# Output projection and beginning of a hybrid SSD and DeltaNet layer: more buffers, earlier gate rows, later halos

## The chip, the cores and the metric

The kernel runs on one core of a Trainium2 chip. The metric is the device time of one execution in microseconds (us); of several executions the median is given. The core has TensorE (PE, with its weight loads listed apart as PEld), VectorE (DVE), ScalarE (ACT), GpSimd (POOL) and SyncE (SP), which here issues most of the DMAs.

## The reference

One decoder layer on a prompt (1024 tokens) and on 64 sample tokens (8 sequences of 8), in float32. The sandwich norms, the SSD scan and the delta rule are those of the usual models; cut to what matters:

```python
mod = silu(c) @ w_ada + b_ada                      # 6 sections of 1024: sh1, sc1, g1, sh2, sc2, g2
h = rms_norm(x, norm_mix_pre) * (1 + sc1) + sh1
proj = h @ w_in                                    # z, x/B/C, dt, q/k/v, gate, beta, alpha
x/B/C, q/k/v = silu(causal_conv4(...))             # the samples bring 3 earlier columns each (halos)
y = gated_rms_norm(ssd_scan(...));  o = gated_rms_norm(delta_rule(...))
m = concat(y, o) @ w_out                           # the output projection, 2048 x 1024
x = x + g1 * rms_norm(m, norm_mix_post)
h = rms_norm(x, norm_ffn_pre) * (1 + sc2) + sh2
x = x + g2 * rms_norm((silu(h @ wg) * (h @ wu)) @ w_down, norm_ffn_post)
```

All states after the step are outputs too: the samples' delta-rule state (8 heads, 8 sequences, 128 x 128) among them.

## The kernel before

Every large product is split into high and low fp32r halves: three matmuls `hi*hi`, `hi*lo`, `lo*hi`. A weight tile of 128x512 is loaded into `wr` by SP, rounded to `wh` by ACT (L164) and its rest taken into `wl` by DVE (L165); pool `wp` has four buffers of each of the three.

The order on PE is that of the program text (a manual schedule). On the other engines and the DMA queues a planner puts the instructions in order, by readiness and priority; `tc.high_priority(n)` shifts it, a negative n backwards. Work beside the matmuls is written as Python generators: `spawn` adds one, and `tick()` lets each go on to its next `yield`, so that its instructions fall between the matmuls. `wait(n)` skips n ticks. Where a loop `while key not in box: tick()` waits, ticks pass with no matmul of the main work between them.

Stages that the change touches:

- The beginning. `ada_block(cb)` (L270) loads four `w2` tiles of 512 KB for one 512-column block of `w_ada` and multiplies them (L268); pool tile `w2` has 8 buffers, which the later `x` tiles share. Blocks 0 and 2, then 1 and 3 give shift and scale of the first norm (`ada_cols`, L287 to L292). `norm_x` (L252 to L254) normalises a row tile of x. `first_half` (L402) transposes x, applies shift and scale (`modulated`, L338 to L349), and does half of the k range of the first two weight tiles, one tick after each three matmuls in its second call. `halos` (L364) loads the samples' earlier conv columns into one buffer `vT` (ACT's queue, L369) and transposes them (L373), five times, one tick apart. `hidden_rest` does the other row tiles. `rates` (L450) multiplies the 32 narrow columns `wst` (L463), and its chain on DVE is read back by L522. `conv_tile` waits in ticks until the halos are done.
- The DeltaNet stage. `ada_rest` (L635) multiplies the other eight blocks of `w_ada`, two halves each, adds them (ACT copy L656, DVE add L658) and stores the sums, not yet folded over partitions, to DRAM (`pdr`).
- The output projection (L1656 to L1718), three groups of row tiles, 16 steps of k each; a step is two halves of 512 columns, each for three row tiles (L1335, L1337, L1338 in `gemm_rows`), with weights from `w_out_half`. Beside group 0 runs `beside`: `rows_late` loads `pdr`, folds the rows into gains (L1301) and into shift and scale of the second norm (L1313), writes the gains to DRAM (L1304) and loads them back broadcast (`load_gains`, L1270 to L1272), and loads the group norm's rates (`RB`). Then `gdn_samples` does the samples' delta rule: per head a state load `s_S` (L1498), products (L1512, L1520, L1530, L1539), the state's decay on POOL (L1527) and a store (L1546). `done` waits in ticks for `rows_late`.

Of the kernel before, what the change touches and what calls it, by code (L numbers as in the profile page):

```python
# [43 lines left out]
def hybrid_step(ctx: ExitStack, tc: tile.TileContext, x_p, x_s, c_p, c_s, st_ssd, st_ssdc, st_gdn, st_gdnc,  # L44
# [30 lines left out]
    pdr = tc.dram_tile([P, 4 * D], F32, name="pdr")  # L75
# [3 lines left out]

    ident = const.tile([P, P], F32, name="ident")  # L80
# [24 lines left out]
    sels = const.tile([P, 4, 9], F32, name="sels")  # L105
    for i in range(4):
        dve.tensor_tensor(out=sels[:, i, :], in0=fold[:, 0:9], in1=ident[:, 9 + i:10 + i].to_broadcast([P, 9]),
                          op=ALU.add)
# [27 lines left out]
    def spawn(gen):  # L136
        tasks.append(gen)
# [19 lines left out]
    def bank():  # L157
        return bg[0].tile([P, 512], F32, name="ps")


    def split_half(src, low=dve):
# [6 lines left out]
    def load_half(src, low=dve):  # L168
# [4 lines left out]
        return split_half(wr, low)  # L173
# [67 lines left out]
    def load_x(i, q=sp):  # L241
        n = P if i < NC else NS
        if i >= 4:
            xts.append(init.tile([P, 2, 512], F32, name="w2", bufs=8).rearrange("p a n -> p (a n)"))
        xt = xts[i]
        q.dma_start(out=xt[0:n], in_=x_p[i * P:(i + 1) * P, :] if i < NC else x_s)
# [22 lines left out]

    def ada_block(cb, between=None):  # L270
        ps = bank()
        for k in range(0, KD, 2):
            w2 = init.tile([P, 2, 512], F32, name="w2", bufs=8)
            sp.dma_start(out=w2, in_=w_ada[k * P:(k + 2) * P, cb * 512:(cb + 1) * 512]
                         .rearrange("(a p) n -> p a n", p=P))
# [153 lines left out]

    wsr = gk.tile([P, 4, NS], F32, name="sm").rearrange("p a t -> p (a t)").rearrange("p (k m) -> p k m", m=32)  # L430
    act.dma_start(out=wsr[:, :, 0:16], in_=w_in[:, C_DT:C_DT + 16].rearrange("(k p) m -> p k m", p=P))
    act.dma_start(out=wsr[:, :, 16:24], in_=w_in[:, C_ALPHA:C_ALPHA + 8].rearrange("(k p) m -> p k m", p=P))
    act.dma_start(out=wsr[:, :, 24:32], in_=w_in[:, C_BETA:C_BETA + 8].rearrange("(k p) m -> p k m", p=P))
    wst = gk.tile([P, NP], F32, name="gate")[:, 0:KD * 64].rearrange("p (k m) -> p k m", m=64).bitcast(F32R)
    pool.memset(wst.bitcast(F32), 0.0)
    act.copy(wst[:, :, 0:32], wsr)
    dve.tensor_sub(wst[:, :, 32:64], wsr, wst[:, :, 0:32].bitcast(F32))

# [3 lines left out]
    first_half(1)  # L442

# [10 lines left out]
    def rates():  # L454
# [180 lines left out]
    def ada_rest():  # L635

        wx = pools["wx"]
# [7 lines left out]

        w4 = load(0)
        sp.dma_start(out=pdr[9:10, :], in_=b_ada[:, 4 * 512:])
        for i in range(16):
            yield from wait(13)
            cb, hf = divmod(i, 2)  # L650
            ps = bank()
            for a in range(4):
                pe.matmul(ps[32 * a:32 * a + 32], lhsT=caF[:, 4 * hf + a, :], rhs=w4[:, a, :], start=True, stop=True)
            if hf == 0:
                pr = wx.tile([P, 512], F32, name="pr")
                act.copy(pr, ps)  # L656
            else:
                dve.tensor_tensor(out=pr, in0=ps, in1=pr, op=ALU.add)  # L658
                for r in (slice(0, 9), slice(10, P)):
                    sp.dma_start(out=pdr[r, cb * 512:(cb + 1) * 512], in_=pr[r])  # L660
            if i < 15:
                w4 = load(i + 1)

# [598 lines left out]
    ph_p = ExitStack()  # L1262
    pre = ph_p.enter_context(tc.tile_pool(name="pre", bufs=1, side="right", reuse_waits="tile"))
# [10 lines left out]
    def rows_late():  # L1274
        def rows(s):
            r = pre.tile([P, D], F32, name="rows2", bufs=2)
            sp.dma_start(out=r, in_=pdr[:, s * D:(s + 1) * D])
            return r


        r0, r1_ = rows(0), rows(1)
# [5 lines left out]
        rw = pre.tile([2 * NT, P], F32, name="rw")  # L1287
        dve.tensor_copy(rw, ps[0:2 * NT, 0:P])
        sp.dma_start(out=rsdr.rearrange("g c p -> (g c) p"), in_=rw)
        for g in range(2):  # L1290
            sp.dma_start(out=RB[g], in_=rsdr[g].rearrange("c p -> (c p)")[0:T].partition_broadcast(P))
        yield from wait(8)
        late_box["RB"] = clock[0]

        def gain_rows(i, r):
            g9 = mid.tile([P, D], F32, name="hv", bufs=5)[0:9]
            sp.dma_start(out=g9, in_=(n_mix_post, n_ffn_post)[i][0].partition_broadcast(9))
            for hf in range(2):
                cs = slice(hf * 512, hf * 512 + 512)
                ps = bank()  # L1300
                pe.matmul(ps[0:9], lhsT=sel, rhs=r[:, cs], start=True, stop=True)  # L1301
                dve.tensor_tensor(out=g9[:, cs], in0=ps[0:9], in1=g9[:, cs], op=ALU.mult)
                yield
            sp.dma_start(out=gaindr[i], in_=g9)  # L1304

        yield from gain_rows(0, r0)
        load_gains(0, GP[0], GS[0])
        r2_ = rows(2)
        ps = bank()
        pv = ps[:, 0:2 * KD * 9].rearrange("p (s k n) -> p s k n", s=2, n=9)  # L1310
        for s_, r_ in ((0, r1_), (1, r2_)):
            for k in range(KD):
                pe.matmul(pv[:, s_, k, :], lhsT=r_[:, k * P:(k + 1) * P], rhs=sel, start=True, stop=True)  # L1313
            if s_ == 0:
                r3 = rows(3)
            yield from wait(1)
        dve.tensor_copy(modT, pv)
        dve.scalar_tensor_tensor(out=modT[:, 1], in0=modT[:, 1], scalar=1.0,
                                 in1=W_FFN.unsqueeze(2).to_broadcast([P, KD, 9]), op0=ALU.add, op1=ALU.mult)
        yield from gain_rows(1, r3)  # L1320
        late_box["rows"] = clock[0]

# [87 lines left out]
    def gdn_samples():  # L1410
# [17 lines left out]
        yield from wait(3)  # L1428
# [66 lines left out]
        for h in range(HG):  # L1495
            hc = 16 + h
# [9 lines left out]
            yield from wait(1)  # L1506
# [11 lines left out]
            yield from wait(1)  # L1518
# [8 lines left out]
            pool.tensor_tensor(out=S0, in0=S0, in1=ge.to_broadcast([P, NB, P]), op=ALU.mult)  # L1527
# [33 lines left out]
    def beside():  # L1561
        yield from rows_late()
        ph_p.close()
        yield from gdn_samples()

# [20 lines left out]
    spawn(beside())  # L1586
# [72 lines left out]
    def w_out_half(k, hf):  # L1659
        return load_half(w_out[k * P:(k + 1) * P, hf * 512:hf * 512 + 512])  # L1660

    ph_f = ExitStack()
    for gi, grp in enumerate(GRP):
# [3 lines left out]
        def done(i, rows, f, hv):  # L1667
# [3 lines left out]
            while "rows" not in late_box:  # L1671
                tick()
# [241 lines left out]
```

## Time and profile before

| what | us |
|---|---|
| median of 3 runs | 2021.33 (2020.7 to 2026.5) |
| profiled execution | 2017.53 |
| its span, first to last instruction | 2015.8 |
| PE busy | 1951.3 |
| DVE busy | 1356.6 |
| ACT busy | 1014.1 |
| POOL busy | 138.7 |

The profile is of one execution. Matmuls are pipelined and overlap in the records, so a busy PE can still be slowed by its clock or by small waits. In a row of the waits the figures are the total in us, the number of waits and the longest.

### The profile page before, as it was taken

How to read it: one execution, taken by the hardware profiler on the slowest of the kernel's cores; microseconds unless marked ns; L12 is line 12 of the kernel's file. 1: busy time of each engine (PE TensorE's matmuls, PEld its weight loads, DVE VectorE, ACT ScalarE, POOL GpSimd, SP SyncE). 2: the span in 40 equal slices, each digit the busy share in tenths (PEclk: the TensorE clock that was granted, in tenths of full speed). 3: DMA queues.
4: the chain of work that ended last, by engine and by line, in shares of the span. 5: the costliest groups of instructions: out<-in, count | busy, mean ns of one | idle time of the engine just before them, and what ended most of it. 6: DMA issues, size and time to landing. Idle time of an engine off the chain costs nothing.

```text
span 2015.8 us, 35469 instructions
## 1 busy us (share of the span) xinstructions
PE 1951.3 (97%) x13211; PEld 1752.5 (87%) x13211; DVE 1356.6 (67%) x2949; ACT 1014.1 (50%) x2515; POOL 138.7 (7%) x188
## 2 busy tenths in 40 slices
PE   6999999999999999999989999999999999999998
PEld 4888999999999998998857677899999999988886
DVE  4768677877887656867648777885555556645465
ACT  3555445555555447767424556753333334444454
POOL 2110000000000001010002210100000000000000
PEclk8999999999999999999989999999999999999999
DMA  9133223333221237545376866422222223633131
GB/s 315 40 92 92 84 92 98 108 95 99 84 58 55 69 92 201 159 121 155 113 218 193 253 203 194 140 75 81 73 78 81 75 82 124 225 125 113 46 100 50
DMA packets 224764, 239.49 MB, mean 119 GB/s; under 512 B 19128, under 2 KB 177387, under 8 KB 224461
## 3 DMA queue, kind: packets, MB, share of 16 engines
q1 hardware_dynamic: 218203, 231.88, 37.2%
q10 hardware_dynamic: 6386, 5.33, 0.8%
q8 instruction: 104, 1.70, 0.4%
q14 instruction: 71, 0.58, 0.1%
HBM read 190.93 MB, written 46.25 MB: 118 GB/s over the span
## 4 chain that ended last, share of the span: by engine, by line
PE 79%; DVE 9%; DMA 6%; ACT 3%; issue 2%; POOL 0%; SPq 0%; DVEq 0%; POOLq 0%; ACTq 0%
PE ps L189 8%; PE ps L190 8%; PE ps L191 8%; PE ps L1815 7%; PE ps L1817 7%; PE ps L1816 7%; PE ps L1335 7%; PE ps L1338 6%; PE ps L1337 6%; PE ps L671 2%; PE ps L725 1%; DMA L<-accr 1%; DVE tm L827 1%; DVE rr L829 1%; DMA mx<-mixdr 1%
## 5 line engine op out<-in xcount | busy, mean ns | idle before, releaser
L189 PE MATMUL ps<-hh,wh 128*128 128x384 f32 (+1 forms) x1232 | 436.2, 354 | 0.0
L190 PE MATMUL ps<-hl,wh 128*128 128x384 f32 (+1 forms) x1232 | 403.3, 327 | 0.0
L191 PE MATMUL ps<-hh,wl 128*128 128x384 f32 (+1 forms) x1232 | 403.3, 327 | 0.0
L1335 PE MATMUL ps<-wh,sh 128*128 128x512 f32 x678 | 275.2, 406 | 7.2 <-ACT wh L164 6.4
L1338 PE MATMUL ps<-wl,sh 128*128 128x512 f32 x678 | 267.3, 394 | 3.9 <-DVE wl L165 3.8
L189 PEld LDWEIGHTS ps<-hh,wh 128*128 128x128 f32 x1232 | 232.3, 189 | 16.8 <-issue 10.4
L1337 PE MATMUL ps<-wh,sl 128*128 128x512 f32 x604 | 238.9, 395 | 0.0
L190 PEld LDWEIGHTS ps<-hl,wh 128*128 128x128 f32 x1232 | 232.4, 189 | 0.8
L191 PEld LDWEIGHTS ps<-hh,wl 128*128 128x128 f32 x1232 | 231.3, 188 | 0.0
L164 ACT CAST wh<-wr 128x512 fp32r<-128x512 f32 x200 | 123.7, 621 | 183.0 <-PE ps L190 87.6
L165 DVE TENSOR_TENSOR wl<-wr,wh 128x512 fp32r<-128x512 f32 x200 | 137.6, 693 | 66.5 <-ACT wh L164 65.8
L1335 PEld LDWEIGHTS ps<-wh,sh 128*128 128x128 f32 x678 | 128.4, 189 | 49.7 <-issue 13.7
L165 DVE TENSOR_TENSOR wl<-wd,wh 128x512 fp32r<-128x512 f32 x130 | 89.6, 692 | 118.0 <-ACT wh L164 114.7
L1338 PEld LDWEIGHTS ps<-wl,sh 128*128 128x128 f32 x678 | 128.4, 189 | 35.2 <-DVE wl L165 6.3
L164 ACT CAST wh<-wd 128x512 fp32r<-128x512 f32 x130 | 80.7, 621 | 138.9 <-PE ps L1337 100.7
L1337 PEld LDWEIGHTS ps<-wh,sl 128*128 128x128 f32 x604 | 114.7, 190 | 21.3
L1815 PE MATMUL ps<-T_0h,wh 128*128 128x272 f32 x352 | 102.2, 290 | 4.3 <-DVE u L1831 1.8
L1752 ACT CAST wh<-s 128x512 fp32r<-128x512 f32 x104 | 64.3, 620 | 78.2 <-PE ps L1816 72.6
L1817 PE MATMUL ps<-T_0h,wl 128*128 128x272 f32 x352 | 102.0, 290 | 0.7 <-DVE wl L1753 0.7
L1815 PE MATMUL ps<-T_1h,wh 128*128 128x272 f32 x352 | 102.1, 290 | 0.0
L1816 PE MATMUL ps<-T_0l,wh 128*128 128x272 f32 x352 | 101.5, 288 | 0.0
L1817 PE MATMUL ps<-T_1h,wl 128*128 128x272 f32 x352 | 101.5, 288 | 0.0
(490 smaller groups left out, 4372.8 us busy)
## 6 DMA issues: line engine op xcount, KB each, us to landing
wr<-in_w_in_dram SPq DMA_DIRECT2D x104, 256.0 KB
wr<-in_w_gate_up_dram SPq DMA_DIRECT2D x104, 256.0 KB
wr<-in_w_out_dram SPq DMA_DIRECT2D x96, 256.0 KB
w<-in_w_ada_dram SPq DMA_DIRECT2D x16, 1024.0 KB
wd<-in_w_down_dram SPq DMA_DIRECT2D x22, 512.0 KB
actdr<-as SPq DMA_DIRECT2D x18, 544.0 KB
L<-accr SPq DMA_DIRECT2D x16, 544.0 KB
am<-actdr SPq DMA_DIRECT2D x44, 192.0 KB
```

Source lines behind the costliest of these rows:

```text
L164: act.copy(wh, src)
L165: low.tensor_tensor(out=wl, in0=src, in1=wh.bitcast(F32), op=ALU.subtract)
L189: pe.matmul(out, lhsT=hi[k], rhs=xh[k], start=(k == 0), stop=False)
L190: pe.matmul(out, lhsT=hi[k], rhs=xl[k], start=False, stop=False)
L191: pe.matmul(out, lhsT=lo[k], rhs=xh[k], start=False, stop=(k == KD - 1))
L1335: pe.matmul(o, lhsT=sh[:, cs], rhs=wh, start=first, stop=False)
L1337: pe.matmul(o, lhsT=sl[:, cs], rhs=wh, start=False, stop=False)
L1338: pe.matmul(o, lhsT=sh[:, cs], rhs=wl, start=False, stop=last)
L1752: act.copy(wh, opa[p])
L1815: pe.matmul(o, lhsT=wh[:, cs], rhs=bh[:, m, :], start=(m == 0 and not on), stop=False, **on)
L1816: pe.matmul(o, lhsT=wh[:, cs], rhs=bl[:, m, :], start=False, stop=False, **on)
L1817: pe.matmul(o, lhsT=wl[:, cs], rhs=bh[:, m, :], start=False, stop=(m == 3), **on)
```

## The change

In the beginning, `w2` gets 12 buffers and the loads are issued ahead in the order block 0, block 2, first weight halves, block 1, and block 3 after block 0's products; a tiny Silu comes first on ACT; the normalising of the later x tiles gets a lower priority; the halos' transposes come three ticks after their load; the narrow weight columns are loaded by SP after `first_half(1)` instead of by ACT before it, and split inside `rates`. In the DeltaNet stage `ada_rest` folds each block at once, into gains (`gaindr`) or into `modT`, with the bias added on DVE; `pdr` is gone. In the output projection odd k take weights from a second pool `wo` of three buffers; `rows_late` keeps only the gains' loads and `RB`, the latter now on POOL's queue; `gdn_samples` starts beside it, issues each head's state load and copies one head ahead, and scales the state on ACT, 8 instructions per head.

```diff
-    sels = const.tile([P, 4, 9], F32, name="sels")      # and 8 instead of 4 in its loop
+    warm = const.tile([1, 1], F32, name="warm")
+    dve.memset(warm, 0.0)
+    act.activation(out=warm, in_=warm, func=AF.Silu)
...
+    def load_ada(cb):                                   # the loads of ada_block, w2 with bufs=12
...
     def halos():
             act.dma_start(out=st, in_=src[:, :, a * P:(a + n) * P].rearrange("b t c -> (b t) c"))
+            yield from wait(3)
             ps = bank()
...
     def hidden_rest():
-        for i in range(3, NT):
-            norm_x(i)
+        with tc.high_priority(-80):
+            for i in range(3, NT):
+                norm_x(i)
...
+    load_ada(0)
+    load_ada(2)
+    for load in loads:
+        load(0)
+    load_ada(1)
     rows = ada_block(0)
+    load_ada(3)
     for i in range(3):
         norm_x(i)
     rows2 = ada_block(2, lambda: ada_cols(0, rows))
-    for load in loads:
-        load(0)
...
     first_half(1)
+    wsr = gk.tile([P, 4, NS], F32, name="sm")...
+    sp.dma_start(out=wsr[:, :, 0:16], in_=w_in[:, C_DT:C_DT + 16]...)     # three, were on act before first_half(1)
...
     def rates():
+        act.copy(wst[:, :, 0:32], wsr)
+        dve.tensor_sub(wst[:, :, 32:64], wsr, wst[:, :, 0:32].bitcast(F32))
+        yield from wait(2)
...
     def ada_rest():
+        b8 = wx.tile([P, 512], F32, name="b8")
+        pool.memset(b8, 0.0)
+        sp.dma_start(out=b8[9:17, :], in_=b_ada[0, 4 * 512:].rearrange("(r c) -> r c", c=512))
         for i in range(16):
-            yield from wait(13)
+            yield from wait(11)
             ...
-            if hf == 0:
-                act.copy(pr, ps)
-            else:
-                dve.tensor_tensor(out=pr, in0=ps, in1=pr, op=ALU.add)
-                for r in (slice(0, 9), slice(10, P)):
-                    sp.dma_start(out=pdr[r, cb * 512:(cb + 1) * 512], in_=pr[r])
+            dve.tensor_tensor(out=pr, in0=ps, in1=pr if hf else b8, op=ALU.add)
+            if hf == 0:
+                continue
+            yield from wait(3)
+            ps = bank()
+            if sec in (0, 3):
+                pe.matmul(ps[0:9], lhsT=sels[:, cb, :], rhs=pr, start=True, stop=True)
+                dve.tensor_tensor(out=g9, in0=ps[0:9], in1=g9, op=ALU.mult)
+                sp.dma_start(out=gaindr[sec // 3][:, 512 * half:512 * half + 512], in_=g9)
+                continue
+            for a in range(4):
+                pe.matmul(pv[:, a, :], lhsT=pr[:, a * P:(a + 1) * P], rhs=sels[:, cb, :], start=True, stop=True)
+            # into modT[:, 0] or, with 1 + and the norm's weight, modT[:, 1]
...
+    wo = ph_b.enter_context(tc.tile_pool(name="wo", bufs=3, side="right", reuse_waits="tile"))
     def rows_late():
-        r0, r1_ = rows(0), rows(1)
+        load_gains(0, GP[0], GS[0])
         ...
-        sp.dma_start(out=rsdr..., in_=rw)               # RB's loads likewise
+        pool.dma_start(out=rsdr..., in_=rw)
-        yield from gain_rows(0, r0)                     # and all that follows it
...
     def gdn_samples():
-        yield from wait(3)
+        yield from wait(16)
...
+        nxt = prep(0)                                   # state load and diagonal copies of a head
+        yield from wait(2)
         for h in range(HG):
+            S0, kb = nxt
...
-            yield from wait(1)
+            if h + 1 < HG:
+                nxt = prep(h + 1)
+            yield from wait(2)
             ...
-            pool.tensor_tensor(out=S0, in0=S0, in1=ge.to_broadcast([P, NB, P]), op=ALU.mult)
+            for b in range(NB):
+                act.activation(out=S0[:, b, :], in_=S0[:, b, :], func=AF.Copy, scale=ge[:, b])
...
-    spawn(beside())
+    spawn(rows_late())
+    spawn(gdn_samples())
     def w_out_half(k, hf):
-        return load_half(w_out[k * P:(k + 1) * P, hf * 512:hf * 512 + 512])
+        return load_half(w_out[k * P:(k + 1) * P, hf * 512:hf * 512 + 512], wp=wo if k % 2 else wp)
         def done(i, rows, f, hv):
-            while "rows" not in late_box:
-                tick()
```

## Rows read from the trace of the kernel before

**Rows 1.** The page's first part: busy us, share of the span and instructions of each engine.

```profile
PE 1951.3 (97%) x13211; PEld 1752.5 (87%) x13211; DVE 1356.6 (67%) x2949; ACT 1014.1 (50%) x2515; POOL 138.7 (7%) x188
```

**Rows 2.** Waits of PE from 0 to 75 us: total us, times, longest us.

```profile
PE ps L259 <- ACT gate L229: 7.5, 1, 7.5
PE ps L373 <- DMA vT<-in_state_ssd_conv_dram: 4.5, 1, 4.5
PE ps L409 <- DVE hl L349: 3.3, 2, 2.2
PE ps L268 <- DMA w<-in_w_ada_dram: 1.7, 2, 1.4
```

**Rows 3.** Windows: busy us and instructions of PE, PEld, DVE, ACT, POOL; clock; DMA.

```profile
44.00:48.00 4.00, 4.00 (x16) 3.21 (x14) 2.33 (x7) 2.38 (x6) 2.95 (x4) 0.60 1.16 212
...
54.00:58.00 4.00, 3.96 (x23) 3.57 (x23) 2.05 (x5) 1.95 (x3) 0.39 (x1) 0.57 0.10 25
...
60.00:90.00 30.00, 29.41 (x184) 25.88 (x185) 23.38 (x56) 18.80 (x44) 7.39 (x10) 1.00 0.13 32
```

**Rows 4.** Timeline of the beginning: start us, us, instruction, idle time before it.

```profile
5.01 1.28 ACT L229 ACT_TABLE_LOAD   x1 [5.01 <-DMA gate<-in_c_sample_dram]
...
20.77 3.81 ACTq L300 DMA_DIRECT2D r<-in_norm_mix_pre_dram  x1
...
41.11 0.75 DVE L254 TENSOR_SCALAR kq<-kq,rs 128x1024 f32<-128x1024 f32 x1 [0.66 <-POOL rs L122]
...
109.19 0.59 PE L522 MATMUL ps<-s,ones 128*128 128x192 f32 x2 [2.34 <-DVE s L516]
```

**Rows 5.** Groups of the DeltaNet stage: count, busy us, mean ns, idle us before.

```profile
L658 DVE TENSOR_TENSOR pr<-ps,pr 128x512 f32<-128x512 f32 x8 | 5.4, 677 | 3.1 <-PE ps L653 3.1
```

**Rows 6.** Groups of PE in the output projection, the moved products.

```profile
L1301 PE MATMUL ps<-rows,sels 128*9 128x512 f32 x8 | 5.0, 706 | 0.0
L1313 PE MATMUL ps<-sels,rows 128*128 128x9 f32 x32 | 3.8, 255 | 1.0 <-DMA rows<-pdr 1.0
```

**Rows 7.** Waits of PE from 990 to 1266 us.

```profile
PE ps L1335 <- ACT wh L164: 6.4, 2, 6.1
PE ps L1338 <- DVE wl L165: 3.8, 2, 2.7
PE ps L1520 <- DVE s_Y L1515: 1.4, 1, 1.4
PE ps L1530 <- DVE s_ut L1522: 1.3, 1, 1.3
PE ps L1597 <- DVE s_S L1542: 1.0, 1, 1.0
```

**Rows 8.** Timeline of SP's queue in the output projection.

```profile
1026.85 6.52 SPq L1272 DMA_DIRECT2D gs<-gaindr  x8
...
1036.97 0.26 SPq L1304 DMA_DIRECT2D gaindr<-hv  x1
...
1039.31 0.84 SPq L172 DMA_DIRECT2D wr<-in_w_out_dram  x2
```

**Rows 9.** Windows of the output projection, columns as in rows 3.

```profile
1030.00:1034.00 4.00, 4.00 (x11) 1.51 (x11) 0.82 (x3) 0.00 (x0) 0.00 (x0) 0.57 0.49 161
...
1044.60:1051.00 6.40, 6.38 (x19) 4.99 (x20) 5.37 (x10) 4.54 (x14) 0.00 (x0) 0.52 0.91 301
1240.00:1247.00 7.00, 6.03 (x19) 4.80 (x20) 6.49 (x14) 2.80 (x5) 0.00 (x0) 0.76 0.58 182
```

**Rows 10.** Durations of one line, ns min/median/max: state scaling on POOL, ACT.

```profile
L1527 POOL TENSOR_TENSOR s_S<-s_S,s_eg x8: 1913/1943/2359, 1078.6 to 1172.1; 128x1024 f32<-128x1024 f32 x8
...
L1156 ACT ACTIVATE h<-h,eb x64: 385/390/414, 786.8 to 994.9; 128x128 f32<-128x128 f32 x64
```

**Rows 11.** Groups of ACT from 990 to 1266 us, the weight casts.

```profile
L164 ACT CAST wh<-wr 128x512 fp32r<-128x512 f32 x94 | 58.0, 620 | 78.6 <-PE ps L1337 33.7 <-issue 23.6 <-DMA wr<-in_w_out_dram 5.9
```

**Rows 12.** Waits of SP's queue over the span.

```profile
SPq L1498 <- DMA out_dram<-s_S: 10.8, 5, 3.2
```

More of the change, by code (lines that the diff above doesn't have):

```diff
@@ L103, in hybrid_step @@
     dve.tensor_add(fold, fold, ident[:, 96:128])
-    sels = const.tile([P, 4, 9], F32, name="sels")
-    for i in range(4):
+    sels = const.tile([P, 8, 9], F32, name="sels")
+    for i in range(8):
         dve.tensor_tensor(out=sels[:, i, :], in0=fold[:, 0:9], in1=ident[:, 9 + i:10 + i].to_broadcast([P, 9]),
@@ L158, in bank, with split_half @@
         return bg[0].tile([P, 512], F32, name="ps")
-    def split_half(src, low=dve):
+    def split_half(src, low=dve, wp=wp):
         wh = wp.tile([P, 512], F32R, name="wh")
@@ L166, in split_half, with load_half @@
         return wh, wl
-    def load_half(src, low=dve):
+    def load_half(src, low=dve, wp=wp):
         wr = wp.tile([P, 512], F32, name="wr")
@@ L172, in load_half @@
         sp.dma_start(out=wr.rearrange("p (a b) -> p a b", b=sh[2]) if len(sh) == 3 else wr, in_=src)
-        return split_half(wr, low)
+        return split_half(wr, low, wp)
     def load_tile(w, c0, low=dve):
@@ L243, in load_x @@
         if i >= 4:
[L244 removed]
+            xts.append(init.tile([P, 2, 512], F32, name="w2", bufs=12).rearrange("p a n -> p (a n)"))
         xt = xts[i]
@@ L268, in ada_rows @@
             pe.matmul(ps[r], lhsT=caF[:, k, :], rhs=w(k), start=k < 4, stop=k >= 4)
+    w2s = {}
+    def load_ada(cb):
+        w2s[cb] = []
+        for k in range(0, KD, 2):
+            w2 = init.tile([P, 2, 512], F32, name="w2", bufs=12)
+            sp.dma_start(out=w2, in_=w_ada[k * P:(k + 2) * P, cb * 512:(cb + 1) * 512]
+                         .rearrange("(a p) n -> p a n", p=P))
+            w2s[cb].append(w2)
     def ada_block(cb, between=None):
@@ L272, in ada_block @@
         for k in range(0, KD, 2):
-            w2 = init.tile([P, 2, 512], F32, name="w2", bufs=8)
-            sp.dma_start(out=w2, in_=w_ada[k * P:(k + 2) * P, cb * 512:(cb + 1) * 512]
-                         .rearrange("(a p) n -> p a n", p=P))
+            w2 = w2s[cb][k // 2]
             ada_rows(ps, lambda k: w2[:, k % 2, :], (k, k + 1))
@@ L442, in hybrid_step @@
     first_half(1)
+    wsr = gk.tile([P, 4, NS], F32, name="sm").rearrange("p a t -> p (a t)").rearrange("p (k m) -> p k m", m=32)
+    sp.dma_start(out=wsr[:, :, 0:16], in_=w_in[:, C_DT:C_DT + 16].rearrange("(k p) m -> p k m", p=P))
+    sp.dma_start(out=wsr[:, :, 16:24], in_=w_in[:, C_ALPHA:C_ALPHA + 8].rearrange("(k p) m -> p k m", p=P))
+    sp.dma_start(out=wsr[:, :, 24:32], in_=w_in[:, C_BETA:C_BETA + 8].rearrange("(k p) m -> p k m", p=P))
+    wst = gk.tile([P, NP], F32, name="gate")[:, 0:KD * 64].rearrange("p (k m) -> p k m", m=64).bitcast(F32R)
+    pool.memset(wst.bitcast(F32), 0.0)
     dcol = cA.tile([P, KD], F32, name="dcol")
@@ L644, in load @@
             return w4
+        b8 = wx.tile([P, 512], F32, name="b8")
+        pool.memset(b8, 0.0)
         w4 = load(0)
-        sp.dma_start(out=pdr[9:10, :], in_=b_ada[:, 4 * 512:])
+        sp.dma_start(out=b8[9:17, :], in_=b_ada[0, 4 * 512:].rearrange("(r c) -> r c", c=512))
         for i in range(16):
-            yield from wait(13)
+            yield from wait(11)
             cb, hf = divmod(i, 2)
+            sec, half = divmod(cb, 2)
             ps = bank()
@@ L1274, in rows_late @@
     def rows_late():
[L1275 to L1278, printed above, removed]
-        r0, r1_ = rows(0), rows(1)
+        load_gains(0, GP[0], GS[0])
         while "norm" not in rate_box:
@@ L1286, in rows_late @@
         pe.transpose(ps[0:2 * NT, 0:P], rsg.rearrange("p g c -> p (g c)"), ident)
-        rw = pre.tile([2 * NT, P], F32, name="rw")
+        rw = g_.tile([2 * NT, P], F32, name="rw")
         dve.tensor_copy(rw, ps[0:2 * NT, 0:P])
-        sp.dma_start(out=rsdr.rearrange("g c p -> (g c) p"), in_=rw)
+        pool.dma_start(out=rsdr.rearrange("g c p -> (g c) p"), in_=rw)
         for g in range(2):
-            sp.dma_start(out=RB[g], in_=rsdr[g].rearrange("c p -> (c p)")[0:T].partition_broadcast(P))
+            pool.dma_start(out=RB[g], in_=rsdr[g].rearrange("c p -> (c p)")[0:T].partition_broadcast(P))
         yield from wait(8)
         late_box["RB"] = clock[0]
[L1295 to L1304, printed above, removed]
-        yield from gain_rows(0, r0)
[L1307 to L1315, printed above, removed]
-            yield from wait(1)
[L1317 to L1321, printed above, removed]
     GRP = ((0, 1, 2), (3, 4, 5), (6, 7, 8))
@@ L1494, in gdn_samples, with prep @@
         so = small.tile([P, HG], F32, name="s_so", bufs=1)
-        for h in range(HG):
-            hc = 16 + h
+        def prep(h):
             S0 = g_.tile([P, NB, P], F32, name="s_S0", bufs=2)
@@ L1505, in gdn_samples @@
             dve.tensor_tensor(out=diag(1), in0=bt(smp[:, h, 1, :]), in1=bt(eg[:, h, :]), op=ALU.mult)
-            yield from wait(1)
+            return S0, kb
+        nxt = prep(0)
+        yield from wait(2)
+        for h in range(HG):
+            S0, kb = nxt
             pk = bank()
```

28 lines of the change are left out of this document (12 added, 16 removed).

## The prediction

> **What bounds the kernel now.** I read the page's engine shares first, then PE's waits by stage, then windows around the longest waits, last the timeline of the queue behind each wait. The shares say that PE is the bound: 1951.3 us busy of a span of 2015.8 [rows 1]. So at most some 64 us of the span are PE idle, and whatever PE does beside them has to be removed, not moved. What can be won beyond the idle time is time in which PE is busy at its lower clock. In PE's waits of the beginning the reader is to see four: 7.5 us for the first Silu, 4.5 us for a halo's load, 3.3 us for the low half of the normalised input, 1.7 us for w_ada [rows 2]. In those of the output projection: 6.4 us for a weight's high half, 3.8 us for its low half, and three of 1.0 to 1.4 us that belong to the samples' chain [rows 7]. After the long waits the granted clock lies between the two levels of 1.2 and 2.4 GHz: 0.60 and 0.57 of full speed in two stretches of the beginning [rows 3], 0.52 behind the wait at 1044 us [rows 9]. A stretch of s us with PE busy at a share c is worth (1 - c) * s.
>
> **The output projection.** (a) The rows' products leave it: L1301 is 5.0 us and L1313 3.8 us of PE [rows 6], together 8.8. They stood in front of the weights' products, so all of it counts here: -8.8.
>
> (b) SP's queue. The gains' loads start at 1026.85 and run to 1033.4; the store of the second gains goes out at 1036.97, when DVE has made them; only behind it come the weight loads, at 1039.31 [rows 8]. PE then stands 6.1 us for the cast of such a weight [rows 7] and works on at 0.52 of the clock for 6.4 us, which is 0.48 * 6.4 = 3.1 [rows 9]. Before it L1313 waited 1.0 for a row load [rows 6]. In the changed kernel the gains are in DRAM long before, so nothing on SP waits for DVE there, and RB's dependent pair is on POOL's queue. The gains' nine loads, and the samples' three, still stand on SP, some 0.4 to 0.8 us of issue each [rows 8]; at most seven buffered halves of weights, where there were four, lie over that. -1.0 - 6.1 - 3.1 = -10.2. If the cover is gone, all 10.2 stay.
>
> (c) Late weights at group changes: 0.3 us of L1335 (6.4 less 6.1) and 3.8 of L1338 [rows 7], and around the longest of them 0.24 * 7.0 = 1.7 of clock [rows 9]; together 5.8. Casts wait mostly for PE to free a buffer (33.7 of 78.6 us idle) [rows 11], so more buffers let them run ahead. But the low half is made by DVE, which at 1240 to 1247 us is busy 6.49 of 7.0 us [rows 9], and that work is not less. Two thirds: -3.9; between 0 and -5.8.
>
> (d) The samples' chain: 1.4 + 1.3 + 1.0 = 3.7 us of waits [rows 7]. It starts some 13 ticks later after its loads but no longer behind the rows, has two ticks instead of one before the first two products of each head, and is over before group 2. Half: -1.9; between -3.7 and +3.7, since a chain that meets group 0's moments can wait as much again. Preparing a head ahead adds a wait on SP: the state load of the next head needs the store of the one before last. That wait is there already, 10.8 us in five, 3.2 at the longest [rows 12], weight loads queued behind it; I cost the change of it at nothing, hidden by the buffers of (b); bare, it is 3.2 a head.
>
> (e) The state's scaling moves from POOL, 8 of 1.94 us, to ACT, 64 that should be like L1156 of the scan: 0.39 us, so 3.1 us a head and 25.0 in all [rows 10]. Weight casts of 0.62 us [rows 11] can queue behind a block. ACT is half idle [rows 1] and a cast has a lead. I take +3 for these and other new waits; between 0 and 25.
>
> Sum: -8.8 - 10.2 - 3.9 - 1.9 + 3 = -21.8.
>
> **The DeltaNet stage.** The products of (a) arrive here. In 1030 to 1034 us they ran at 0.57 of the clock [rows 9], so 1.7 of the 8.8 were clock, and here they cost 7.1: PE is the bound here too, so +7.1, between 0 (in gaps) and 8.8. DVE gets eight more adds of 0.68 [rows 5], four products of the same shape and small copies, about 9 us; ACT loses eight copies. DVE is 67% busy [rows 1], and the chain of the delta rule can be late by one add: +1.0, between 0 and 9. The DMAs to `pdr`, two per block, go from SP; a load and a store of nine partitions come for four of the blocks: nothing. Sum +8.1.
>
> **The beginning.** (f) The table load is 1.28 us in front of the Silu for which PE waits 7.5 [rows 2, 4]. ACT stands idle 5.01 us before it for the loads of c [rows 4], so the load moves into idle time. But the first product's weights are waited for just after (1.7) [rows 2], and these come no sooner: 0, between -1.3 and +1.3 (ACT issues the loads of c as well, and the table load may come ahead of them).
>
> The Trainium skill (ScalarE: Activation LUTs, What ACT_TABLE_LOAD costs) puts a switch of tables at about 1.28 us of load and 1.38 us of drain. The trace agrees on the load with its 1.28 [rows 4]; the drain no run here shows. By the page the lower end would be -2.7 and the sum 1.4 lower if the weights were early.
>
> (g) L409's waits are 3.3 us [rows 2]; in the longer one DVE does L254, 0.75 us, the normalising of a later tile, ahead of the input's low half, and ACT its square [rows 4]. With low priority these go behind: -1.5, and half of the clock loss behind it, 0.40 * 4 / 2 = 0.8 [rows 3]. Between 0 and -4.9. What is late next: the later tiles, now closer to their transposes.
>
> (h) Halos. Each load went out when the transposes before it freed `vT`, and its own transposes stood next but three matmuls on PE: 4.5 us of wait [rows 2], then 0.43 * 4 = 1.7 at 0.57 of the clock [rows 3]. With three more ticks, some 24 matmuls of the main work lie between; at the pace of 60 to 90 us, 29.41 us for 184 [rows 3], about 4 us. -4.5 - 1.7. Then PE reaches the second and third row tiles sooner than DVE has made them: a new wait, nearest L409's 3.3 [rows 2]; +2.0, between 0 and 3.3.
>
> (i) The first conv tile waits for the fifth halo, now due some 15 ticks later, so that ticks pass without matmuls and `rates` and its chain on DVE move up on PE, with two conv tiles of DVE work behind them. L522 waits 2.3 today [rows 4]: +1.0; between -2.3 and +7.5, the longest wait of this stage [rows 2].
>
> (j) Loads. Twelve `w2` buffers let block 1 go out without waiting for block 0's products, and the narrow columns no longer share the queues with it. PE meets blocks 1 and 3 only behind `first_half(0)`, where it waits 1.7 us for w_ada in all [rows 2]: 0, between -1.7 and +3.8, since a parameter load already held ACT's queue for 3.81 us [rows 4] and fuller queues can do so in front of ACT's part of the input.
>
> Sum: -2.3 - 6.2 + 2.0 + 1.0 = -5.5.
>
> **In all** -21.8 + 8.1 - 5.5 = -19.2. The profiled execution took 2017.53, of which the span is 2015.8, so it becomes 1998.3. The median of the runs shown is 2021.33, 3.8 above that execution; the forecast is for a median: 2002.1.
>
> **The rivals.**
> 1. All waits named go. Output projection -8.8 - 10.2 - 5.8 - 3.7 = -28.5; DeltaNet +7.1; beginning -3.3 - 1.6 - 4.5 - 1.7 - 2.3 = -13.4: -34.8, so 1986.5. For it: ACT and DVE have idle time on average [rows 1]. Against: at the group changes DVE has none [rows 9].
> 2. The beginning gives its waits back. The new wait of (h) is 3.3 and that of (i) 7.5: -2.3 - 6.2 + 10.8 = +2.3 there, -11.4 in all, 2009.9. For it: the halos only change place, and the ticks that the conv tile waits are empty. Against: 24 matmuls now stand between load and use.
> 3. It doesn't do what it says: SP still holds the weights, now behind nine gain loads and the samples' loads, and the 10.2 of (b) stay: -9.0, 2012.3. For it: eight of those took 6.52 us [rows 8]. Against: some of that was waiting, and there are more buffers.
> 4. Slower: ACT. In each head the eight scalings, 3.1 us [rows 10], stand ahead of a cast that PE needs, and PE waits them out and runs on slowly as at 1240 us, 1.7 more [rows 9]: 8 * 4.8 = 38.4 in place of the +3, so -19.2 - 3 + 38.4 = +16.2, 2037.5. It decides against the change from 22.2 / 38.4 of that, about 1.8 of the 3.1 us bare in each head. For it: PE has stood for a cast before [rows 7]. Against: the casts' lead [rows 11], now larger. The Trainium skill says that ACT is a strict first-in first-out queue (TensorE: Matmul & The Clock Gate, Architectural detail); by that rule a cast planned behind the block cannot pass it. No row here shows a cast behind such a block.
>
> **How the numbers follow.** The forecast has 0.60, rival 1 0.14, rival 2 0.12, rival 3 0.07, rival 4 0.07. Within 0.3%, 6.1 us, is what a measurement of this kernel can't tell from no change. Rivals 2 and 3 reach into that with 0.03 each, the forecast's tail with 0.02: same 0.08; slower 0.07; faster 0.85. The range leaves out half of rival 1 below and rival 4 with the tails of 2 and 3 above: 1988 to 2014.
>
> **What would show it.** (a), (b): no L1301 or L1313 after 990 us, no wait of 6 us for a cast, SP's weight loads even through 1026 to 1039 us; PE's idle time from 990 to 1266 us down from about 15 to 5. (c): no wait over 1 us for `wl` at the group changes. (d), (e): the sample heads before 1190 us, their products with waits under 1 us, casts not late behind scalings. (h): no wait over 1 us at the halos' transposes, main products about 6 us earlier. (i): L522's wait near 3. Wrong would be: a cast or `wl` waited for once per head, a wait at the fifth halo, or PE's clock low in a new place.

## The result and the profile after

The changed kernel takes 2035.18 us (median of 6 runs, 2031.0 to 2036.5), the kernel before 2023.91 beside it. The ratio is 1.0056, interval 1.0039 to 1.0073: slower by 11.3 us, where 19.2 less was forecast. The profiled execution has 2036.45 us and a span of 2034.6; that of the kernel before, 2017.53, was a quick one, so single profiles are read here for places, and medians for prices.

The page's first part: engines' busy time, share of the span, instructions.

```profile
PE 1966.1 (97%) x13211; PEld 1762.8 (87%) x13211; DVE 1354.7 (67%) x2964; ACT 1041.3 (51%) x2582; POOL 123.3 (6%) x184
```

PE has as many instructions as before [rows 1] and is busy 14.8 us longer. So some of the loss is no wait: either the clock or the products themselves are slower.

Waits of PE in the changed kernel: from 0 to 75 us, 75 to 120, and 1005 to 1285 (total us, times, longest).

```profile
PE ps L261 <- ACT gate L231: 6.4, 1, 6.4
PE ps L270 <- DMA w<-in_w_ada_dram: 2.6, 3, 1.5
PE ps L384 <- DVE ht L350: 2.3, 1, 2.3
PE ps L421 <- DVE hl L359: 1.0, 3, 0.4
...
PE ps L539 <- DVE s L533: 2.9, 1, 2.9
PE ps L384 <- DMA vT<-in_state_gdn_conv_dram: 2.9, 1, 2.9
...
PE ps L1341 <- ACT wh L166: 18.2, 1, 18.2
PE ps L1457 <- DVE s_ko L1443: 2.9, 1, 2.9
PE ps L1343 <- DVE sl L1354: 2.3, 1, 2.3
PE ps L1523 <- POOL r L1399: 1.3, 1, 1.3
PE ps L1533 <- DVE s_Y L1526: 0.6, 1, 0.6
```

Against [rows 2] the first Silu, the low half (L421) and the first halo are waited for less, and a later halo 2.9 us. It is the fourth of the five, and the chain has its load (start us, us, what):

```profile
77.31 6.92 DMA vT<-in_state_gdn_conv_dram
```

Against [rows 7] the 6.4 us for casts and the 3.8 us for low halves are gone, and one wait of 18.2 us for a cast stands at the second k of the output projection. The chain says what it was:

```profile
1016.87 3.20 DMA mixdr<-y
1020.21 4.71 DMA gp<-gaindr
1025.74 5.56 DMA s_d<-accr
...
1034.53 0.59 ACT wh L166
1035.16 0.80 PE ps L1341
```

On ACT's timeline (idle time before an instruction in brackets) the samples' exp, L1432, stands ahead of three weight casts that have nothing to do with it, and waits 13.8 us for its operand:

```profile
1032.60 1.28 ACT L1432 ACT_TABLE_LOAD   x1 [13.78 <-DVE s_d L1431]
1033.90 0.63 ACT L1432 ACTIVATE s_d<-s_d 64x512 f32<-64x512 f32 x1
1034.49 1.99 ACT L166 CAST wh<-wr 128x512 fp32r<-128x512 f32 x3
```

SP's timeline says why that operand is late, and the weights of k = 9 too:

```profile
1016.87 0.32 SPq L1213 DMA_DIRECT2D mixdr<-y  x1
1017.34 0.33 SPq L1289 DMA_DIRECT2D mx<-mixdr  x1
1017.94 1.15 SPq L174 DMA_DIRECT2D wr<-in_w_out_dram  x2
1020.21 0.33 SPq L1309 DMA_DIRECT2D gp<-gaindr  x1
1020.63 4.57 SPq L1311 DMA_DIRECT2D gs<-gaindr  x8
1025.29 0.35 SPq L1418 DMA_DIRECT2D smx<-smdr  x1
1025.74 0.63 SPq L1426 DMA_DIRECT2D s_d<-accr  x1
1026.42 0.62 SPq L1428 DMA_DIRECT2D s_eg<-eaccr  x1
1027.09 2.03 SPq L174 DMA_DIRECT2D wr<-in_w_out_dram  x3
```

The loads for k = 9 go out at 1017.94, behind the last store of the scan (L1213), since k = 9 now uses the new odd-k buffers; PE is out of work at 1017.0. The gains come next, then the exp's operand. A window (columns as in [rows 3]) bounds the exp's share of the 18.2 us:

```profile
1024.50:1025.70 1.20, 0.00 (x0) 0.00 (x0) 0.00 (x0) 0.00 (x0) 0.00 (x0) 0.50 0.00 0
```

The DMA engines move nothing there, so the first weights of k = 9 had landed by 1024.5 us. Up to then, 7.5 us, late weights can explain the wait; from then until their cast at 1034.5 us, 10 us, it is the exp alone.

After both waits, for the halo and for the rates, the clock is low again:

```profile
84.00:92.00 8.00, 7.63 (x33) 5.76 (x34) 5.08 (x9) 2.83 (x5) 0.00 (x0) 0.60 0.20 53
108.00:116.00 8.00, 5.05 (x18) 3.81 (x17) 4.53 (x13) 1.05 (x3) 0.02 (x1) 0.68 0.01 3
```

Last, a place where nothing was changed: w_down took 4.6 us longer in the profile (270.7 to 275.2 us from its first product to the end) without a new wait. From start to start a 512-column product took 229.0 ns in it before and 233.3 ns after (worked out from the starts of neighbouring products, those over 1.15 times the median left out).

### The profile page after: what moved, and what is told of

It reads as the page before. It is cut to its first block, busy times and chain, and to the rows that moved or that the text cites. A ratio compares the mean times of both kernels' runs of the same rounds, so it can differ in the third digit from the quotient of the medians.

```text
span 2034.6 us, 35499 instructions
## 1 busy us (share of the span) xinstructions
PE 1966.1 (97%) x13211; PEld 1762.8 (87%) x13211; DVE 1354.7 (67%) x2964; ACT 1041.3 (51%) x2582; POOL 123.3 (6%) x184
## 3 DMA queue, kind: packets, MB, share of 16 engines
q0 software_dynamic: 320, 1.12, 0.2%
## 4 chain that ended last, share of the span: by engine, by line
PE 80%; DVE 8%; DMA 5%; ACT 4%; issue 2%; POOL 1%; SPq 0%; ACTq 0%; DVEq 0%; POOLq 0%
PE ps L191 8%; PE ps L1341 8%; PE ps L1823 7%; PE ps L1825 7%; PE ps L1824 7%; PE ps L1344 7%; PE ps L192 7%; PE ps L193 7%; PE ps L1343 7%; PE ps L711 2%; PE ps L765 1%; DVE tm L867 1%; DMA wr<-in_w_in_dram 1%; DVE rr L869 1%; DVE uc L861 1%
## 5 line engine op out<-in xcount | busy, mean ns | idle before, releaser
L1341 PE MATMUL ps<-wh,sh 128*128 128x512 f32 x678 | 276.4, 408 | 18.9 <-ACT wh L166 18.2
L1824 PE MATMUL ps<-T_1l,wh 128*128 128x272 f32 x352 | 101.7, 289 | 0.0
```

The source lines that it names most:

```text
L1341: pe.matmul(o, lhsT=sh[:, cs], rhs=wh, start=first, stop=False)
L1824: pe.matmul(o, lhsT=wh[:, cs], rhs=bl[:, m, :], start=False, stop=False, **on)
```

## The experiments

**The parts alone.** Each part of the change on the kernel before, with a pad in the constants (two lines that allocate and clear it) that keeps the buffers behind it at their old addresses modulo 256 bytes:

```
+    pad = const.tile([P, 32], F32, name="pad")     # 128 bytes for the output projection, 224 for the beginning
+    pool.memset(pad, 0.0)
```

> The kernel before with the output projection's part of the change alone (odd-k buffers, early gate rows, samples' chain); a pad keeps every later buffer at the address modulo 256 bytes that it had before. Theory A (the samples' exp, waiting on ACT for its load, holds the weights' casts): the wait of about 18 us for a cast at the first products of k = 9 is here in full, so the output projection's stage stays within 2 us of the 269.2 us of before, and the 7 to 9 us of moved products appear before it: +4 to +9 us on the median of before. Rival B (the changed beginning spoils the planner's order later on): the wait of 18 us is not here, the stage falls by about 20 us and the kernel is 10 to 15 us faster than before. w_down: at 229 ns from start to start of a 512-column product if the rate hangs on the addresses, 233 ns if it comes with this part of the change.

2022.27 us, ratio 0.9993 (0.9973 to 1.0014). The wait for the cast is there, so rival B falls: the output projection's part makes it by itself.

```profile
PE ps L1325 <- ACT wh L165: 18.6, 1, 18.6
```

Its first product comes 5.1 us later than in the kernel before, its stage is 1.3 us shorter, w_down stays at 229.0 ns.

> The kernel before with the beginning's part alone (twelve buffers, later halos, early table load, later rates), padded to the old addresses modulo 256 bytes. Theory C (the fifth halo's load now lands in ticks without matmuls, and the clock falls behind it and at the rates): PE's idle time from 60 to 200 us grows by 5 to 9 us, some of it is given back later where PE waited for others; +4 to +11 us on the median of before. Rival (these waits exist only together with the early gate rows): the beginning is 3 to 6 us shorter, -3 to -6 us. The output projection keeps its waits of 6 and 4 us; w_down 229 ns if the rate hangs on addresses, 233 ns if it comes with this part.

2024.30 us, ratio 0.9997 (0.9977 to 1.0018): neither. Its profile has the main products 9.6 us behind at 245 us, and 4.8 of that is given back at 780 us, where PE waited before; the median shows none of the rest. Theory C had a halo's load as the cause, and in this profile PE waits for none: from 40 to 120 us it waits 2.4 us for the rates, 1.9 for `ht` and 1.8 for the low half, and the clock is at 0.69 and 0.63 in the two stretches from 50 to 70 us (0.66 and 1.00 before).

**The addresses.** The change adds 160 bytes to the constants (four more `sels`, `warm`), and the weights' buffers `wh` and `wl` move by as much.

```
+    pad = const.tile([P, 40], F32, name="pad")     # before, 160 bytes more and nothing else
```

> The kernel before with 160 bytes per partition put in front of the constants, as many as the change adds, and nothing else: the weights' buffers move from 32 to 192 modulo 256 bytes while the activations' halves stay. Theory D (the matmul's rate hangs on the addresses of its operands): w_down's 512-column products go from 229 to 233 ns from start to start, its stage by 4 to 5 us, the 272-column products of the up projection from 125.6 to 126.2 ns, the DeltaNet stage's 384-column ones from 175 to 174 ns: between 0 and +4 us in all. Rival (the rate is another thing, as the granted clock of the execution or the work beside it): no stage moves by more than 1 us, 0 in all.

2033.39 us, ratio 1.0038 (1.0017 to 1.0058): 7.7 us slower for 160 unused bytes. w_down 233.3 ns, 275.4 us. By the medians alone it is 9.6 us. Theory D holds, and its price is larger than expected. In the profile the output projection took 5.1 us more too; its products went from 229.8 to 233.2 ns, which for some 830 of them is an estimated 2.8 us. The rest need not be the rate: in the run with 96 bytes above w_down's activations, below, that stage is 5.6 us longer at 229.9 ns.

```
+    pad = const.tile([P, 24], F32, name="pad")     # the changed kernel, 96 more: 256 in all
```

> The changed kernel with 96 more bytes per partition in front of the constants, so that the weights' buffers stand at 32 modulo 256 bytes again; nothing else differs. Theory D (the addresses cost what the shift alone cost, 0.38% on the median, 4.7 us of them in w_down): w_down's 512-column products at 229 ns, its stage at 270.5 us, the wait of 18 us unchanged; -6 to -10 us against the changed kernel, 2025 to 2029 us, within 0.3% of the kernel before. Rival (the changed kernel's 0.56% are its waits alone): no stage but w_down moves, at most -4.7 us, 2030 to 2035 us.

2026.67 us, ratio 1.0013 (0.9997 to 1.0029): 8.5 us less than the changed kernel, and 229.0 ns. The wait of 17.9 us for the cast is still there. So, by these medians, most of the 0.56% are addresses. In the groups of PE from 1800 to 1950 us (busy us, mean ns) it is a slower product without idle time; the changed kernel, then this one:

```profile
L1344 PE MATMUL ps<-wl,sh 128*128 128x512 f32 x216 | 85.4, 396 | 0.0
L1341 PE MATMUL ps<-wh,sh 128*128 128x512 f32 x216 | 85.4, 395 | 0.0
```

```profile
L1343 PE MATMUL ps<-wh,sh 128*128 128x512 f32 x221 | 86.6, 392 | 0.0
L1346 PE MATMUL ps<-wl,sh 128*128 128x512 f32 x221 | 85.9, 389 | 0.1
```

The next five ask which address counts; each is a single execution (2034.67, 2030.66, 2032.82, 2024.94 and 2024.70 us in the order below), too few for a time, and is read for the rate alone. They pad the kernel before by 64, 32 or 224 bytes in the constants, or put 96 bytes above w_down's activations (`sh`, `sl`), or both that and the 160:

```
+    padr = ctx.enter_context(tc.tile_pool(name="padr", bufs=1, side="right", reuse_waits="tile")).tile([P, 24], F32, name="padr")
+    pool.memset(padr, 0.0)
     stk = ctx.enter_context(tc.tile_pool(name="stk2", bufs=3, side="right", reuse_waits="tile"))
```

> The kernel before with 64 bytes in front of the constants: the weights' buffers stand at 96 modulo 256 bytes, 32 modulo 64 as in the kernel before. If the position within 64 bytes decides the rate (32 fast, 0 slow): w_down's products stay at 229 ns. If that within 256 bytes does, or the distance to the activations' halves (at 224): another rate, 227 to 235 ns.

> The kernel before with 32 bytes in front of the constants: the weights' buffers stand at 64 modulo 256 bytes, 0 modulo 64. If the position within 64 bytes decides: w_down's products at 233 ns, as with 160 bytes. If not: 227 to 231 ns.

232.4 and 233.3 ns: the position within 64 bytes decides nothing.

> The kernel before with 96 bytes put above the activations' halves of w_down alone: there they move from 224 to 128 modulo 256 bytes, the weights' buffers stay at 32; the halves of the output projection stay. If the weights' position alone sets the rate: w_down's products at 229 ns as before. If the distance between the two does (it was 64 modulo 256, and is now 160): another rate, 231 to 235 ns, in w_down alone; the output projection as before.

234.2 ns in w_down, 229.9 in the output projection, where nothing moved.

> The kernel before with the 160 bytes in front of the constants (weights at 192) and the 96 above w_down's activations (at 128 modulo 256), so that in w_down the distance is 64 again, as before, and in the output projection 224, as with the 160 bytes alone. If the distance sets the rate: w_down back at 229 ns, the output projection at 233. If the weights' position does: both at 233 ns.

229.0 ns in w_down, 233.1 in the output projection. Both operands have moved in w_down and the old rate is back; only the weights have in the output projection, and it is slow. The weights' position alone is refuted.

> The kernel before with 224 bytes in front of the constants: the weights' buffers at 0 modulo 256. Of four positions tried 32 gave 229.0 ns, 64 gave 233.3, 96 gave 232.4 and 192 gave 233.3. If whole multiples of 64 are slow with these activations: 233 ns. If 0 is its own case: below 231.

233.3 ns. All of w_down in one table (start to start; address of `wh` less that of `sh`, modulo 256 bytes):

```
distance   32     64     64     96     128    160    224    224
ns         233.3  229.0  229.0  233.3  232.4  234.2  233.3  233.3
kernel     +224   before both   +32    +64    right  +160   after
```

Of six distances one is quick, and the kernel before has it. The differences between the columns are those of the pads; that the kernel before stands at 64 follows from the order and sizes of its tiles and is in no trace.

**The wait for the cast.** Samples' loads eight ticks later, gains' loads behind the rates:

```
-        load_gains(0, GP[0], GS[0])
         while "norm" not in rate_box:
...
         late_box["RB"] = clock[0]
+        load_gains(0, GP[0], GS[0])
...
+        yield from wait(8)
         smx = g_.tile([P, HG, 4, NS], F32, name="smx")
...
-        yield from wait(16)
+        yield from wait(8)
```

> The changed kernel with the samples' loads and exp eight ticks later (the wait behind them eight shorter) and the nine gain loads put behind the rates: four weight halves then stand ahead of them on SP and two casts ahead of the exp on ACT. Theory A (18.2 us at 1035 us are the exp's wait, in front of the casts): the weights of k = 9 go out at 1018 us as now and land some 3 us later, PE waits 4 to 5 us there in place of 18.2 and no wait over 3 us follows: -13 to -16 us against the changed kernel, some 2020 us, level with before. Rival E (SP's queue alone makes it, nine gain loads and three of the samples): the same loads stand somewhere, the wait moves by 8 ticks and stays over 10 us: -2 to -6 us. Rival F (the odd-k buffers come free late and that alone makes the 18 us): no change.

2021.80 us, 13.4 less than the changed kernel; ratio to before 0.9985 (0.9965 to 1.0005). PE's longest wait from 1000 to 1280 us, and ACT's timeline:

```profile
PE ps L1341 <- ACT wh L166: 7.5, 1, 7.5
```

```profile
1024.86 1.27 ACT L166 CAST wh<-wr 128x512 fp32r<-128x512 f32 x2 [5.00 <-DMA wr<-in_w_out_dram]
1033.99 1.28 ACT L1433 ACT_TABLE_LOAD   x1 [7.87 <-DVE s_d L1432]
```

The exp still waits, 7.9 us, but two casts stand ahead of it and PE has their work. Now the cast waits for the weights themselves. F falls as the whole cause, and A stands with a larger rest than its 4 to 5 us: 7.5, as much as the window above left to late weights. That the queue alone did it (E) falls by size, though both are in the chain: the exp's operand was late because of SP. This run moved the exp and the gains' loads together; an exp moved on ACT with SP's order as it is was not run.

The rest is the loads of k = 9. The first four halves go to the four early buffers instead, then the even k to the new ones:

```
+    out_calls = []
     def w_out_half(k, hf):
+        out_calls.append(k)
+        wo_now = k % 2 == 0 and len(out_calls) > 4
...
-... wp=wo if k % 2 else wp)
+... wp=wo if wo_now else wp)
```

> The run with samples and gains late (2021.8 us), but the first four weight halves of the output projection, k = 8 and 9, use the four buffers that are free early, and then the even k the new ones; before, k = 9 took the new buffers, whose loads could go out only behind the last store of the state-space stage. Theory H (what was left of the wait, 7.5 us at 1025 us, is that late load): the wait falls to 0 to 4 us and the stage by as much, -4 to -7 us, 2015 to 2018 us. Rival (SP's queue: the samples' and gains' loads are then what the next halves wait for): the wait only moves on to k = 10 or 11 with over 5 us, 0 to -2 us.

2018.81 us, ratio 0.9970 (0.9952 to 0.9988), 3.0 us less than the run before it. PE's longest waits from 1000 to 1280 us:

```profile
PE ps L1343 <- DVE sl L1354: 4.7, 2, 2.7
PE ps L1341 <- ACT wh L166: 2.0, 2, 1.2
```

Theory H holds for the casts, 7.5 to 2.0 us. Part of it only moved: for the low half of the activations (`sl`), 0.8 us in the run before it, PE now waits 4.7. With the weights' low half, 1.9 to 0.6, these waits fall from 10.2 to 7.3 us, close to the 3.0 of the medians.

**The halos.** On the beginning's part alone, all five loads into free `w2` buffers behind the loads of x, transposes one tick apart:

```
+    def load_halos():
+        for src, a, n in halo_src:
+            st = init.tile([P, 2, 512], F32, name="w2", bufs=12).rearrange("p a n -> p (a n)")[0:24, 0:n * P]
+            sp.dma_start(out=st, in_=src[:, :, a * P:(a + n) * P].rearrange("b t c -> (b t) c"))
+            halo_in.append(st)
```

> The beginning's part alone (as in the run of that part), but the five halos' loads go out on SP behind the loads of x, into free ones of the twelve buffers, and each halo's transposes stand one tick behind the last, as before the change. With the beginning's part alone the main products were 1.3 us ahead at 77 us, 3.7 behind at 96, 9.2 behind at 114 and 9.6 at 245 us. Theory C (the late halos make that: empty ticks and the low clock behind them): no wait for a halo's load, the main products 3 to 6 us ahead at 96 us and level or ahead at 245 us, the first product of the output projection 5 to 9 us earlier than with the beginning's part alone. Rival G (the later rates, with DVE's chain for which PE waits at 108 us, make it): still 5 to 10 us behind at 245 us, no gain over 2 us. Median: 2015 to 2020 by C, 2022 to 2025 by G.

2022.96 us, ratio 1.0001 (0.9983 to 1.0019). The profile does what C said, level at 245 us and 7.0 us earlier at the output projection, but by the median it is 1.3 us less than the beginning's part alone, and by the ratios to the kernel before 0.8 more: not settled here.

**All together,** with and without this, and with the beginning of before:

> The changed kernel with all four corrections: samples and gains late, the first four weight halves in the early buffers, the halos' loads early, and the pad that puts the weights at 32 modulo 256 bytes. If the four causes are separate and add up (about -13 for the casts, -5 for the late halves, -6 for the halos, -7 for the addresses, from 2035): some 2004 us, faster than both kernels by 0.8 to 1.3%. If they cover each other (a wait that goes in one place is waited for in the next): 2010 to 2018 us.

> The kernel with all corrections (2004.05 us) but with the halos as the change has them. In single profiled executions the halos' early loads brought 11.9 us to the beginning's part alone, in its medians only 1.3. Theory C: the halos are worth 4 to 8 us of the median where nothing later waits them out: 2008 to 2012 us. Rival (the beginning varies from execution to execution and the halos are worth nothing that can be measured): 2002 to 2006 us.

> The output projection's part with its two corrections, at the old addresses modulo 256 bytes, and the beginning of the kernel before. Against the kernel with all corrections (2004.05 us) it tells what the corrected beginning brings: 2 to 6 us if it is the 5 us by which its first products of the w_in gemm come earlier (2006 to 2010 us), nothing or less if those are waited out later, at the rates and in the DeltaNet stage (2001 to 2005 us). Against the kernel before it gives the output projection alone: -18 to -22 us if the forecast of -21.8 + 8.1 = -13.7 was too careful, -12 to -15 us if it was right.

2004.05 us, ratio 0.9904 (0.9880 to 0.9928), with all corrections: they add up, and it is faster than both kernels. 2010.70 with the change's late halos (0.9923, 0.9896 to 0.9950). 2009.52 with the beginning of before (0.9907, 0.9878 to 0.9937). So in this pair the early halos are worth 6.7 us by the medians and 3.8 by the ratios, with intervals that overlap; the direction is likely, the size open. The change's own beginning, next to the old one, brings nothing that these runs show. The output projection alone, corrected, is 18.8 us faster than the kernel before by the ratio (interval 12.8 to 24.7) and 14.7 by the medians: both cases expected lie in that.

Waits of PE from 40 to 120 us with early halos, then with late ones:

```profile
PE ps L547 <- DVE s L541: 4.8, 1, 4.8
PE ps L332 <- DVE halT L393: 1.8, 1, 1.8
```

```profile
PE ps L541 <- DVE s L535: 2.8, 1, 2.8
PE ps L386 <- DMA vT<-in_state_gdn_conv_dram: 2.8, 1, 2.8
PE ps L386 <- DVE ht L352: 2.0, 1, 2.0
PE ps L423 <- DVE hl L361: 1.8, 1, 1.8
```

The sums are not far apart, 6.6 and 9.4 us. The rest is seen in the clock, from 50 to 70 us and behind the fourth halo's wait from 80 to 90, early halos first:

```profile
50.00:60.00 10.00, 8.17 (x52) 6.89 (x52) 9.30 (x20) 5.99 (x12) 4.65 (x5) 0.83 0.33 92
60.00:70.00 10.00, 10.00 (x61) 8.51 (x60) 6.87 (x25) 4.34 (x12) 2.56 (x4) 1.00 0.00 0
...
80.00:90.00 10.00, 10.00 (x62) 8.52 (x61) 9.64 (x15) 6.01 (x14) 0.10 (x1) 1.00 0.26 67
```

```profile
50.00:60.00 10.00, 7.94 (x31) 5.62 (x32) 8.64 (x17) 5.24 (x10) 5.35 (x5) 0.62 0.02 7
60.00:70.00 10.00, 10.00 (x42) 7.81 (x41) 4.16 (x16) 3.85 (x10) 1.08 (x2) 0.70 0.00 0
...
80.00:90.00 10.00, 7.22 (x33) 5.43 (x32) 4.53 (x7) 3.03 (x5) 0.00 (x0) 0.66 0.51 134
```

## Why the prediction was wrong

By parts it said -13.7 for the output projection with what it moves to the DeltaNet stage, and -5.5 for the beginning. Alone they measured -1.4 and -0.6 us (0.07% and 0.03%, each uncertain by some 4 us), and the addresses, which it did not have, +7.7. That makes +5.7 of the 11.3; the other 5.6 are within the three intervals and were not traced to the end. One place is seen in single profiles: the wait for the fourth halo stands in the changed kernel and not in the beginning's part alone, and the main products, n-th against n-th, are 12.2 us behind at 114 us in the one and 8.9 in the other.

Three steps failed: the products' time, taken as fixed; the cover of (b), and with it the exp that (e) does not name; the halo's load, whose own time (h) does not have.

- **The term that was missing.** The prediction took every product's duration from before. The tiles that the change adds cost no instruction of the loops, and yet they slow the products of the output projection, the up projection (125.6 to 126.2 ns for 272 columns) and w_down: 7.7 us when added alone, 8.5 when undone, 8.1 between two corrected kernels (2018.81 and 2010.70). None of its rivals had it.
- **(a), the moved products:** right. No product on the rows is left behind 990 us, and in the run of this part alone the stage starts 5.1 us later for +8.1 forecast.
- **(b), SP's queue:** the dependent pair and the store are gone as said, and the cover failed. "At most seven buffered halves of weights, where there were four, lie over that" is the step that broke: at the start of the stage the three new buffers hold nothing, since their loads go out behind the scan's last store, and the old ones hold k = 8 and 10 instead of 8 and 9. More buffers gave less lead at the one place where SP is full.
- **(c), late weights at group changes:** right, no wait for `wl` is left in the list of the changed kernel.
- **(d), the samples' chain:** 2.9 + 1.3 + 0.6 = 4.8 us of waits for 3.7 before; within its bounds, no gain.
- **(e), +3 for new waits and ACT:** mis-sized. The 64 scalings took 387 ns each as priced, and no cast was late behind them. What came was 18.2 us at one cast, 10 of them behind the samples' exp alone, which the part names nowhere although "it starts some 13 ticks later after its loads" speaks of it: the wait of 16 ticks stands behind the exp and moves PE's part alone; the exp itself stayed where its loads put it. The two corrections bring back 16.4 us (13.4 + 3.0).
- **Rival 4** named the right mechanism at the wrong instruction. By the Trainium skill (TensorE: Matmul & The Clock Gate, Architectural detail) ACT is a strict first-in first-out queue; the trace agrees, with three casts behind an exp that waited 13.8 us. It is a wait at the head of the queue that costs, not work: 25 us of scalings cost nothing to be seen, one late operand 10 to 18.
- **Rival 3** was right in part: nine gain loads and the samples' loads do stand in front of the next weights, for 6.9 us (1020.2 to 1027.1).
- **(f)** came near its lower bound, 7.5 to 6.4 us, and w_ada took 0.9 of it; **(g)** right, 3.3 to 1.0; the new wait of **(h)** for `ht` was 2.3 for 2.0 forecast, at the first halo's transposes.
- **(h), -6.2 for the halos:** failed. "With three more ticks, some 24 matmuls of the main work lie between" is right, and so is their time: between the fourth halo's load and its transposes stand 26 products, from 77.3 to 81.4 us. What the term leaves out is how long the load takes. It took 6.9 us, so PE waited 2.9, then the clock was at 0.60 from 84 to 92 us. The kernel before has a halo's load of 5.1 us (from 48.8), more than the cover too, and one of 2.2 us (from 58.3). The DMA engines' busy share was 0.79 to 1.12 from 80 to 83 us in the changed kernel and 0.91 to 1.12 from 48 to 52 before, but 0.05 to 0.18 from 58 to 62 before: the later load seems to have met the loads of the next stage, 1 MB of w_ada from 76.2 and a weight half from 77.7 us. No run moved those, so this is not shown. The fifth halo is not waited for: its load, from 85.4 us, has the rates' products before its transposes at 95.6. That the halos' waits only change place is what rival 2 said. With the loads early the halos are worth 1.3 and 6.7 us in the two pairs of medians, for 6.2 forecast.
- **(i):** 2.9 us for 2.3, within the +1.0; the clock behind it at 0.68.

Corrected, the output projection's part is worth 18.8 us by the ratio and 14.7 by the medians, for 13.7 forecast. The beginning's 5.5 by the medians (2009.52 to 2004.05) equals the 5.5 forecast, but the ratios to the kernel before differ by 0.0003, some 0.6 us, and six runs each do not settle it: the agreement may be luck. The forecast valued what the edits could bring, and gave a chance of 0.07 to their falling into each other's way.

## What to carry to other kernels

A few bytes in an early pool move every tile behind them: when a stage without an edit changes its pace, compare start-to-start times of like products before looking for a wait, and try a pad. Ahead of moving a chain to "later", look at which of its instructions the wait really holds back; on an in-order engine the first one with a late operand holds all that stands behind it. Count the buffers that are full at the moment when the queue is, not those that exist. Hold the work that is to cover a load against the load's time at that place: halos' loads took 2.2, 5.1 and 6.9 us here.

## What was not expected of the hardware

The time of a matmul hung on where its two operands lie to each other in SBUF: 229.0 ns for 512 columns at one distance modulo 256 bytes (64), 232.4 to 234.2 ns at five others, the old rate again when both were moved. The pads move every tile of their side of SBUF along, so that these two operands are the pair that counts is the nearest reading, and not shown for itself. Products of 384 columns went the other way with the 160 bytes, 175.1 to 174.3 ns in the DeltaNet stage. Why, no run here shows.
